# Four changes of queue, engine and order, and the per-head sums of squares of q and k in four column groups

## The chip, the cores and the metric

The kernel runs on one core of a Trainium2 chip. The metric is the device time of one execution in microseconds (us). A core has five engines that work side by side, each through its own instructions in order: TensorE (PE, matrix products; its weight loads are shown apart as PEld), VectorE (DVE), ScalarE (ACT), GpSimd (POOL) and SyncE (SP, which here only issues DMAs). They wait for each other by semaphores. DMAs are issued by SP and ACT (hardware queues) and by POOL (software queue).

## The reference

One decoder layer is computed in float32 for 1024 prompt tokens and 8 sample tokens (1032 columns), with model width 1024 and feed-forward width 2816. The outputs are the new activations and the new caches. Cut to what matters here:

```python
h = h + 0.5 * swiglu(rmsnorm(h, g_f1), w_f1_gu, w_f1_down)      # up 1, down 1
u = rmsnorm(h, g_mix) @ w_in                                     # the mixer's projections
q = rmsnorm(q.reshape(bsz, T, N_HEADS_A, HEAD_DIM), g_q) * (HEAD_DIM ** -0.5)   # per head of 64
k = rmsnorm(k.reshape(bsz, T, N_HEADS_A, HEAD_DIM), g_k)
mix = concat(attention(q, k, v), conv_module(glu), pool_mixer(c)) @ w_out
h = h + mix
h = h + 0.5 * swiglu(rmsnorm(h, g_f2), w_f2_gu, w_f2_down)      # up 2, down 2
```

The rmsnorm of q and k per head needs, for each of the 8 + 8 heads and each of the 1032 tokens, the sum of 64 squares.

## The kernel before

Activations lie transposed: a tile has 128 features on the partitions and tokens along the columns, either a half of 516 columns (`HF`), or a third of 344 (`CH`, `CW` = 344). A float32 product is made of three matmuls on high and low parts (`hi` on ACT by a copy that rounds, `lo` on DVE by a subtraction), and each stage streams its weights: a 256 KB load, a high part and a low part ("wop") for each 128x512 block.

The stages follow each other on PE: **up 1** (L512 to L514), **down 1** (L773 to L775), the **mixer** (projections L283 to L285, then the V blocks L1158 to L1160, with the convolution, the norms of q and k and the attention mixed in), **out-proj** (L283 to L285 again) and **up 2**, **down 2** (the same lines as up 1 and down 1). A scheduler that plans ahead of time turns the program into one fixed instruction order per engine; what is written later in the program with less to wait for can be placed earlier. Hardware DMAs rotate over eight completion slots, so a DMA waits until the one eight before it has landed; those of POOL have eight slots of their own.

*Up.* `up` works with seven products per feed-forward tile f (a Strassen-like scheme on two halves of the features and two halves of the tokens). Products 1 and 2 of the first f's ("early": 14 in up 1, 12 in up 2) need only the raw first half of the tokens, so they run first and their results are copied out of PSUM (`v`, ACT, L521) and kept in DRAM (L522). Product 2 of an f accumulates on product 1 in the same PSUM tile, and stands `lag` f's behind it; there are four such tiles of two banks. Meanwhile `norms()` squares the tokens (ACT, L405), sums the squares over the eight feature tiles on DVE (L407), and `total` sums over the partitions on PE (L388), then a root on ACT (L390) and a reciprocal on DVE (L391). The first halves of x are loaded by SP (L368); `fetch_x` (L380 to L382) loads the second halves, through POOL's queue, into buffers of 13 that rotate; the eighth waits until one comes free. In up 2 the lag is 3 (L888), and its early products are interleaved with the last of out-proj.

*Mixer.* For q and k, eight 128-row tiles are projected. `total` (L1116 to L1119) sums the squares of q tile p and k tile p with a 0/1 matrix `sel`: two matmuls of 344 columns, one into partitions 0 to 31 of `acc[c]`, one into 32 to 63; they accumulate over p = 0 to 3 in three banks (c = 0 to 2), so there are 12 such pairs. `side_v` (L1186 ff.) is a generator that advances one step per V block (16 blocks of 128 tokens by 256 columns). It scales the sums by r, takes root and reciprocal (`stat`, L1198 to L1202), splits the result into `rr` (high part on 64 partitions by ACT, low part on the other 64 by DVE), and `norm(t)` (L1217) spreads it with one product `bcx` x `rr` for each tile and third, and multiplies q or k by that on DVE. Between its steps `conv_tail` is advanced: the layer norm of the convolution, whose sums are matmuls against `ones` (L277) of the split `sh`, `sl` of the two convolution tiles `cy`. `xs` (L1064 to L1068), high plus low part of the eight sample columns, is added up by eight small POOL instructions.

*Out-proj.* Each of 16 steps adds the product to h (L933), stores the sum to `hd2` in DRAM through POOL's queue (L934) and squares it (L935). Up 2 reads `hd2` back.

Of the kernel before, what the change touches and what calls it, by code (L numbers as in the profile page):

```python
# [11 lines left out]
F32 = mybir.dt.float32  # L12
# [8 lines left out]
KT = D // P  # L21
SEQ = 1024
NS = 8
T = SEQ + NS
CW = T // 3
CH = [slice(i * CW, (i + 1) * CW) for i in range(3)]
HT = T // 2
# [159 lines left out]
class Trunk:  # L187
# [151 lines left out]
    def up(self, src, n, g, norm, lag, extra=iter(())):  # L339
# [39 lines left out]

        def fetch_x(k, hf):  # L380
            x = tmp(f"x{hf}")
            nc.gpsimd.dma_start(x, src(k, hf))  # L382
            return x
# [9 lines left out]
        def norms():  # L393
            if not norm:
                for _ in range(2):
                    yield
                total(1, self.tail)
                return
            accs = []
            xs = [fetch_x(k, 1) for k in range(HK)]  # L400
            for hf in range(2):
                acc = None
                for k in range(KT):
                    sq = xs[k] if hf else tmp("sq")
                    nc.scalar.activation(sq, sq if hf else first_x[k], AF.Square)  # L405
                    if k:
                        nc.vector.tensor_tensor(sq, sq, acc, op=ALU.add)  # L407
                    acc = sq
                    if k == HK - 1:
                        yield  # L410
                        if hf == 0:
                            xs += [fetch_x(i, 1) for i in range(HK, KT)]
                accs.append(acc)
                yield
            yield
            for hf in range(2):
                total(hf, accs[hf])
                yield
# [431 lines left out]
    def body(self):  # L850
# [32 lines left out]
        with contextlib.ExitStack() as right:  # L883
            with self.page_pools():
                with self.side_pools():
                    mh, ml = self.mixer(hd)
                self.x1p = right.enter_context(self.first_pool())
                gen = self.up(lambda k, hf: hd2[k][:, HF[hf]], 2, "g2", False, 3)  # L888
                self.out_proj(mh, ml, hd, hd2, gen)
# [7 lines left out]
    def out_proj(self, mh, ml, hd, hd2, ahead):  # L897
# [24 lines left out]
        for at, (hf, d) in enumerate(steps):  # L922
# [4 lines left out]
            for j in range(2):  # L927
# [5 lines left out]
                nc.vector.tensor_tensor(out, ps, out, op=ALU.add)  # L933
            nc.gpsimd.dma_start(hd2[d][:, HF[hf]], x)  # L934
            nc.scalar.activation(sq, x, AF.Square)  # L935
# [15 lines left out]
    def mixer(self, hd):  # L951
# [114 lines left out]
        for k in range(KT):  # L1066
            nc.gpsimd.tensor_tensor(xs[:, k], self.xh[k][:, SEQ:T].bitcast(F32), self.xl[k][:, SEQ:T].bitcast(F32),
                                    op=ALU.add)  # L1068
# [17 lines left out]

        acc = [self.ps()[:, :CW] for _ in range(3)]
        qk = [None] * 8
        wv = None
        pool = self.pool_tail(pooled)  # L1090
        for p in range(4):
# [7 lines left out]
            for c in range(3):  # L1099
# [16 lines left out]
                def total(c=c, p=p, parts=parts):  # L1116
                    for e in range(2):
                        nc.tensor.matmul(acc[c][32 * e:32 * e + 32], sel[:, 32 * p:32 * p + 32], parts[e],
                                         start=p == 0, stop=p == 3)  # L1119

# [63 lines left out]
    def side_v(self, conv, qk, acc, gq, smq):  # L1184
# [9 lines left out]
        yield  # L1194
        sc = [self.t("stat")[0:64] for _ in range(3)]
        for c in range(3):
            r = self.r[0:64, CH[c]]
            nc.vector.tensor_tensor(sc[c], acc[c][0:64], r, op=ALU.mult)  # L1198
            nc.vector.tensor_tensor(sc[c], sc[c], r, op=ALU.mult)
            nc.scalar.activation(sc[c], sc[c], AF.Sqrt, bias=self.eps[0:64])  # L1200
            nc.vector.reciprocal(sc[c], sc[c])
            nc.vector.tensor_tensor(sc[c], sc[c], r, op=ALU.mult)  # L1202
        tail = self.conv_tail()
        next(tail, None)
        yield
        for c in range(3):
            self.hi(rr[0:64, CH[c]], sc[c])
            self.lo(rr[64:128, CH[c]], sc[c], rr[0:64, CH[c]])
        next(tail, None)
        yield  # L1210
        next(tail, None)
        yield

# [486 lines left out]
```

## Time and profile before

| | |
|---|---|
| three timed runs | 1853.35, 1855.25, 1856.14 us, median 1855.25 |
| the profiled execution | 1856.26 us, of which the profile's span is 1854.5 us |
| mean granted PE clock | 0.996 of 2.4 GHz |
| busy: PE, DVE, ACT, POOL | 98%, 72%, 39%, 12% of the span |
| the chain that ended last | PE 90%, DVE 4%, DMA 3%, ACT 2%, issue 1% |

The page says how busy each engine is. With PE busy for 98% of the span, what can be won is in the few gaps where PE waits, in the stretches that run at half clock, and in the work that PE does. The view of the waits lists the gaps by the engine and line waited for; the timeline of an engine shows each instruction with its start, its duration and in brackets the idle time before it.

### The profile page before, as it was taken

To read this page: it belongs to the slowest core of one execution; us is meant where nothing else is said; L and a number is where in the kernel's file an instruction comes from. 1 tells how busy PE (TensorE), PEld (TensorE's weight loads), DVE (VectorE), ACT (ScalarE), POOL (GpSimd) and SP (SyncE) were. 2 spreads that over 40 slices of the span, in tenths; PEclk is the share of its full clock that TensorE was granted. 3 is DMA by queue.
4 is the path that set the end of the run, shared out by engine and by line. 5 is a ranking of instruction groups with operands and counts; after the bars stand their busy time and mean duration, and the time that the engine had idled before them with its cause. 6 is when DMAs were issued, how large, how long until landed. Compare 5 with 4: busy or idle time off the path is not lost.

```text
span 1854.5 us, 35895 instructions
## 1 busy us (share of the span) xinstructions
PE 1822.7 (98%) x14436; PEld 1750.0 (94%) x14436; DVE 1343.4 (72%) x2140; ACT 724.7 (39%) x1307; POOL 213.4 (12%) x205
## 2 busy tenths in 40 slices
PE   7999999999999999999899999999999999999999
PEld 7999999999999999998865689989999999999999
DVE  6877787778686566997666755577777877868654
ACT  6532222322333455235655653443222222243342
POOL 2100000000000004732532423200000000000000
PEclk9999999999999999999999999999999999999999
DMA  9544365454964243212353256654433435596421
GB/s 330 195 139 149 115 182 191 144 183 161 327 244 118 84 158 94 53 38 75 121 159 115 93 170 207 216 169 158 131 127 111 142 120 181 168 325 245 117 81 46
DMA packets 155578, 286.72 MB, mean 155 GB/s; under 512 B 25992, under 2 KB 32732, under 8 KB 155412
## 3 DMA queue, kind: packets, MB, share of 16 engines
q1 hardware_dynamic: 116276, 206.21, 35.7%
q10 hardware_dynamic: 34560, 63.20, 9.1%
q0 software_dynamic: 4576, 15.01, 2.4%
q8 instruction: 113, 1.85, 0.4%
q14 instruction: 53, 0.43, 0.1%
HBM read 208.29 MB, written 78.61 MB: 155 GB/s over the span
## 4 chain that ended last, share of the span: by engine, by line
PE 90%; DVE 4%; DMA 3%; ACT 2%; issue 1%; SPq 0%; ACTq 0%; DVEq 0%
PE ps L512 15%; PE ps L513 15%; PE ps L514 15%; PE ps L773 8%; PE ps L774 8%; PE ps L775 8%; PE ps L283 5%; PE ps L284 5%; PE ps L285 5%; PE ps L1599 2%; PE ps L1580 1%; DMA wr<-wgu 1%; PE ps L1527 1%; DVE pt L1530 1%; PE ps L1528 1%; PE ps L1159 1%
## 5 line engine op out<-in xcount | busy, mean ns | idle before, releaser
L512 PE MATMUL ps<-xot,wop 128*128 128x258 f32 x1408 | 396.3, 283 | 1.8 <-DVE v L565 1.8
L513 PE MATMUL ps<-xot,wop 128*128 128x258 f32 x1408 | 397.9, 283 | 0.0
L514 PE MATMUL ps<-xot,wop 128*128 128x258 f32 x1408 | 397.0, 282 | 0.0
L773 PE MATMUL ps<-mop,wop 128*128 128x258 f32 x1232 | 348.1, 283 | 0.9 <-DVE v L578 0.9
L774 PE MATMUL ps<-mop,wop 128*128 128x258 f32 x1232 | 347.4, 282 | 0.0
L775 PE MATMUL ps<-mop,wop 128*128 128x258 f32 x1232 | 346.6, 282 | 0.0
L512 PE MATMUL ps<-xo,wop 128*128 128x258 f32 x1056 | 301.3, 286 | 6.1 <-ACT v L521 3.9
L513 PE MATMUL ps<-xo,wop 128*128 128x258 f32 x1056 | 300.0, 284 | 0.0
L514 PE MATMUL ps<-xo,wop 128*128 128x258 f32 x1056 | 299.6, 284 | 0.4 <-DVE wop L244 0.4
L512 PEld LDWEIGHTS ps<-xot,wop 128*128 128x128 f32 x1408 | 265.1, 189 | 2.9 <-issue 2.6
L513 PEld LDWEIGHTS ps<-xot,wop 128*128 128x128 f32 x1408 | 265.8, 189 | 1.5 <-issue 1.5
L514 PEld LDWEIGHTS ps<-xot,wop 128*128 128x128 f32 x1408 | 265.9, 189 | 0.0
L774 PEld LDWEIGHTS ps<-mop,wop 128*128 128x128 f32 x1232 | 233.5, 190 | 0.0
L773 PEld LDWEIGHTS ps<-mop,wop 128*128 128x128 f32 x1232 | 232.2, 189 | 1.1 <-issue 1.1
L775 PEld LDWEIGHTS ps<-mop,wop 128*128 128x128 f32 x1232 | 232.7, 189 | 0.0
L241 ACT ACTIVATE wop<-s 128x512 fp32r<-128x512 f32 x176 | 105.8, 628 | 292.6 <-DVE s L478 227.9
L512 PEld LDWEIGHTS ps<-xo,wop 128*128 128x128 f32 x1056 | 201.1, 191 | 9.0 <-ACT v L521 5.5
L514 PEld LDWEIGHTS ps<-xo,wop 128*128 128x128 f32 x1056 | 201.2, 191 | 0.9 <-DVE wop L244 0.8
L513 PEld LDWEIGHTS ps<-xo,wop 128*128 128x128 f32 x1056 | 201.4, 191 | 0.3 <-DVE xo L374 0.2
L244 DVE TENSOR_TENSOR wop<-wr,wop 128x512 fp32r<-128x512 f32 x180 | 121.7, 696 | 55.1 <-ACT wop L241 54.9
L244 DVE TENSOR_TENSOR wop<-s,wop 128x512 fp32r<-128x512 f32 x176 | 117.7, 688 | 36.1 <-ACT wop L241 35.6
L241 ACT ACTIVATE wop<-wr 128x512 fp32r<-128x512 f32 x180 | 107.2, 622 | 89.1 <-PE ps L775 76.7
(263 smaller groups left out, 3404.8 us busy)
## 6 DMA issues: line engine op xcount, KB each, us to landing
wr<-wgu SPq DMA_DIRECT2D x227, 256.0 KB
mt<-v ACTq DMA_DIRECT2D x88, 258.0 KB
mr<-mt SPq DMA_DIRECT2D x88, 258.0 KB
m<-v ACTq DMA_DIRECT2D x66, 258.0 KB
mr<-m SPq DMA_DIRECT2D x66, 258.0 KB
kept<-v ACTq DMA_DIRECT2D x52, 258.0 KB
v<-kept SPq DMA_DIRECT2D x52, 258.0 KB
h<-hd SPq DMA_DIRECT2D x48, 258.0 KB
```

The source lines that it names most:

```text
L241: self.nc.scalar.activation(out, src, AF.Copy)
L244: (eng or self.nc.vector).tensor_tensor(out, src, hi.bitcast(F32), op=ALU.subtract)
L283: mm(out, wh, xh, start=i == 0, stop=False)
L284: mm(out, wh, xl, start=False, stop=False)
L285: mm(out, wl, xh, start=False, stop=i == n - 1)
L512: mm(out, wh, xh, start=start and k == 0, stop=False)
L513: mm(out, wh, xl, start=False, stop=False)
L514: mm(out, wl, xh, start=False, stop=stop and k == HK - 1)
L773: mm(out, wh, mh, start=opens, stop=False)
L774: mm(out, wh, ml, start=False, stop=False)
L775: mm(out, wl, mh, start=False, stop=closes)
L1599: mm(O[half[e], q1 - w:q1], vt[j // 2][:, j % 2, hc:hc + 64], pT[:, e, :], start=j == 0, stop=j == 2 * b + 1)
```

## The change

1. In up 1, `norms()` loads the second half of x (eight loads) through SP's queue; every other user of `fetch_x` stays on POOL's.
2. In up 2 the lag is 2, not 3.
3. The 16 stores of out-proj into `hd2` are issued by ACT.
4. The eight additions of `xs` are done by DVE.
5. `total` for q and k makes four matmuls of 172 columns, into the four groups of 32 partitions of `acc[c]`: q and k, first half of the third and second half. The statistics then stand on 128 partitions by 172 columns: root and reciprocal are one instruction each per third as before, with half the columns; the multiplications with r are made by 64 partitions; the high part goes into a tile `stath` first and from there by two copies on ACT to `rr`; the low part is two subtractions. `conv_tail` is still advanced once with the statistics, and then four times before the first norm where it was twice; `rr` is written just ahead of the first of these four, so each norm stands two V blocks later.

```diff
-        def fetch_x(k, hf):
+        def fetch_x(k, hf, queue=nc.gpsimd):
             x = tmp(f"x{hf}")
-            nc.gpsimd.dma_start(x, src(k, hf))
+            queue.dma_start(x, src(k, hf))
...
-            xs = [fetch_x(k, 1) for k in range(HK)]
+            xs = [fetch_x(k, 1, nc.sync) for k in range(HK)]
...
-                            xs += [fetch_x(i, 1) for i in range(HK, KT)]
+                            xs += [fetch_x(i, 1, nc.sync) for i in range(HK, KT)]
...
-                gen = self.up(lambda k, hf: hd2[k][:, HF[hf]], 2, "g2", False, 3)
+                gen = self.up(lambda k, hf: hd2[k][:, HF[hf]], 2, "g2", False, 2)
...
-            nc.gpsimd.dma_start(hd2[d][:, HF[hf]], x)
+            nc.scalar.dma_start(hd2[d][:, HF[hf]], x)
...
-            nc.gpsimd.tensor_tensor(xs[:, k], self.xh[k][:, SEQ:T].bitcast(F32), self.xl[k][:, SEQ:T].bitcast(F32),
+            nc.vector.tensor_tensor(xs[:, k], self.xh[k][:, SEQ:T].bitcast(F32), self.xl[k][:, SEQ:T].bitcast(F32),
...
-        acc = [self.ps()[:, :CW] for _ in range(3)]
+        acc = [self.ps()[:, :CH2] for _ in range(3)]
...
-                    for e in range(2):
-                        nc.tensor.matmul(acc[c][32 * e:32 * e + 32], sel[:, 32 * p:32 * p + 32], parts[e],
-                                         start=p == 0, stop=p == 3)
+                    for g in range(4):
+                        nc.tensor.matmul(acc[c][32 * g:32 * g + 32], sel[:, 32 * p:32 * p + 32],
+                                         parts[g % 2][:, g // 2 * CH2:(g // 2 + 1) * CH2],
+                                         start=p == 0, stop=p == 3, skip_group_check=True)
...
-        sc = [self.t("stat")[0:64] for _ in range(3)]
+        sc = [self.t("stat") for _ in range(3)]
+        half = [slice(0, 64), slice(64, 128)]
...
         for c in range(3):
-            r = self.r[0:64, CH[c]]
-            nc.vector.tensor_tensor(sc[c], acc[c][0:64], r, op=ALU.mult)
-            nc.vector.tensor_tensor(sc[c], sc[c], r, op=ALU.mult)
-            nc.scalar.activation(sc[c], sc[c], AF.Sqrt, bias=self.eps[0:64])
-            nc.vector.reciprocal(sc[c], sc[c])
-            nc.vector.tensor_tensor(sc[c], sc[c], r, op=ALU.mult)
+            x = sc[c][:, 0:CH2]
+            for h in range(2):
+                nc.vector.tensor_tensor(x[half[h]], acc[c][half[h]], self.r[half[h], cols(c, h)], op=ALU.mult)
+                nc.vector.tensor_tensor(x[half[h]], x[half[h]], self.r[half[h], cols(c, h)], op=ALU.mult)
+            nc.scalar.activation(x, x, AF.Sqrt, bias=self.eps)
+            nc.vector.reciprocal(x, x)
+            for h in range(2):
+                nc.vector.tensor_tensor(x[half[h]], x[half[h]], self.r[half[h], cols(c, h)], op=ALU.mult)
...
         for c in range(3):
-            self.hi(rr[0:64, CH[c]], sc[c])
-            self.lo(rr[64:128, CH[c]], sc[c], rr[0:64, CH[c]])
-        next(tail, None)
-        yield
-        next(tail, None)
-        yield
+            x, xh = sc[c][:, 0:CH2], self.t("stath", dt=F32R)[:, 0:CH2]
+            self.hi(xh, x)
+            for h in range(2):
+                nc.scalar.activation(rr[0:64, cols(c, h)], xh[half[h]].bitcast(F32), AF.Copy)
+                self.lo(rr[64:128, cols(c, h)], x[half[h]], xh[half[h]])
+        for _ in range(4):
+            next(tail, None)
+            yield
```

Lines of the changed kernel stand 1 lower than before from the top, 2 lower at the statistics' first lines and 11 lower from `norm` on (L407 is L408, L1217 is L1228).

Three places in the order move. The first is DVE in up 1, around the sums of squares of the second half of x (`x_289` to `x_345`, each x its own buffer; `sq` are the sums of the first half; `wop` the low parts of weights). Before:

```order
L407 TENSOR_TENSOR x_339<-x_339,x_293 128x516
L244 TENSOR_TENSOR wop<-wr,wop 128x512 x2
L407 TENSOR_TENSOR x_341<-x_341,x_339 128x516
L391 RECIPROCAL r<-sd 128x516
L244 TENSOR_TENSOR wop<-wr,wop 128x512 x2
L407 TENSOR_TENSOR x_343<-x_343,x_341 128x516
L244 TENSOR_TENSOR wop<-wr,wop 128x512 x2
L407 TENSOR_TENSOR x_345<-x_345,x_343 128x516
L391 RECIPROCAL r<-sd 128x516
```

After, at the same place:

```order
L408 TENSOR_TENSOR x_339<-x_339,x_293 128x516
L408 TENSOR_TENSOR x_341<-x_341,x_339 128x516
L245 TENSOR_TENSOR wop<-wr,wop 128x512
L408 TENSOR_TENSOR x_343<-x_343,x_341 128x516
L245 TENSOR_TENSOR wop<-wr,wop 128x512
L408 TENSOR_TENSOR x_345<-x_345,x_343 128x516
L245 TENSOR_TENSOR wop<-wr,wop 128x512
L392 RECIPROCAL r<-sd 128x516
L245 TENSOR_TENSOR wop<-wr,wop 128x512 x4
L392 RECIPROCAL r<-sd 128x516
```

The last sum now stands ahead of the first reciprocal, and two low parts, not six, stand between `x_339` and it.

The second is SP's queue at the start (`x_174` to `x_186` are the first halves of x, `v` the kept products read back). Before:

```order
L368 DMA x_183<-x 128x516 x2
L368 DMA x_186<-x 128x516 x2
L465 DMA wr<-wgu 128x512 x38
L532 DMA v_1357<-kept_0_158 128x516
L532 DMA v_1359<-kept_0_158 128x516
```

After, from the last of the seven loads of x that follow the first nine weight loads:

```order
L383 DMA x_343<-x 128x516
L466 DMA wr<-wgu 128x512 x2
L383 DMA x_345<-x 128x516
L466 DMA wr<-wgu 128x512 x27
L533 DMA v_1357<-kept_0_158 128x516
```

The eight loads of x stand among the weights, and 27 weight loads stand behind the eighth.

The third is ACT in `side_v`, from the load of the root's table on (`stat` the root, `misc` and `v` belong to the V blocks, `sh` the convolution's high parts, `rr` the statistics' high parts). Before:

```order
L241 ACTIVATE sh<-cy_8947 128x344
L1165 ACTIVATE misc<-ps 128x1
L1200 ACT_TABLE_LOAD
L1200 ACTIVATE stat<-stat,eps 64x344
L241 ACTIVATE sh<-cy_9462 128x344
L1166 ACTIVATE v_10030<-ps,misc 128x256
L241 ACTIVATE wboth<-wr 128x512
L1200 ACTIVATE stat<-stat,eps 64x344
L241 ACTIVATE sh<-cy_8947 128x344
```

After:

```order
L1208 ACT_TABLE_LOAD
L1208 ACTIVATE stat<-stat,eps 128x172 x3
L1167 ACTIVATE misc<-ps 128x1
L1168 ACTIVATE v_10048<-ps,misc 128x256
L1167 ACTIVATE misc<-ps 128x1
L1168 ACTIVATE v_10049<-ps,misc 128x256
L242 ACTIVATE stath<-stat 128x172
L1219 ACTIVATE rr<-stath 64x172 x2
L242 ACTIVATE stath<-stat 128x172 x2
L242 ACTIVATE sh<-cy_8947 128x344
```

The first `sh` stood ahead of the table load; it now stands behind the three `stath`, which need the statistics' last multiplications. On PE the matmul that reads this `sh` still stands right behind the third V block; the first norm (L1217, now L1228) moved from behind the fourth V block to behind the sixth.

## Rows read from the trace of the kernel before

**Rows 1.** Engines' busy time, from the page: us, share of the span, instructions.

```profile
PE 1822.7 (98%) x14436; PEld 1750.0 (94%) x14436; DVE 1343.4 (72%) x2140; ACT 724.7 (39%) x1307; POOL 213.4 (12%) x205
```

**Rows 2.** Waits of PE: line, waited-for engine and line, us, times, longest.

```profile
PE ps L388 <- DVE x L407: 5.7, 1, 5.7
PE ps L1217 <- DVE rr L244: 5.5, 3, 4.0
PE ps L512 <- ACT v L521: 3.9, 8, 0.7
```

**Rows 3.** Timeline of PE in up 1: start, duration, instruction, idle before.

```profile
35.56 0.28 PE L514 MATMUL ps<-xo,wop 128*128 128x258 f32 x1
41.58 2.06 PE L388 MATMUL ps<-x,mat 128*128 128x258 f32 x4 [5.74 <-DVE x L407]
```

**Rows 4.** Windows: stretch, busy time and count by engine, granted PE clock, DMA share, GB/s.

```profile
core 0: us, PE busy (x) PEld busy (x) DVE busy (x) ACT busy (x) POOL busy (x), PEclk, DMA share, GB/s
10.00:20.00 10.00, 9.84 (x71) 9.61 (x70) 5.93 (x9) 6.39 (x12) 0.81 (x2) 1.00 1.04 390
40.00:50.00 10.00, 8.42 (x46) 8.08 (x47) 5.59 (x6) 1.81 (x3) 1.07 (x2) 0.66 0.53 177
886.60:893.60 7.00, 5.44 (x20) 4.71 (x21) 4.80 (x8) 3.67 (x7) 3.86 (x4) 0.51 0.26 91
```

**Rows 5.** Timeline of DVE in up 1, around the sums of x.

```profile
32.58 0.69 DVE L407 TENSOR_TENSOR x<-x,x 128x516 f32<-128x516 f32 x1
...
34.50 3.38 DVE L391 RECIPROCAL r<-sd 128x516 f32<-128x516 f32 x1 [1.23 <-ACT sd L390]
...
40.75 0.69 DVE L407 TENSOR_TENSOR x<-x,x 128x516 f32<-128x516 f32 x1
```

**Rows 6.** Timelines of ACT and POOL in up 1: a copy out, the eighth load.

```profile
30.82 0.60 ACT L521 ACTIVATE v<-ps 128x516 f32<-128x516 f32 x1
...
19.57 0.54 POOL L382 DMA_DIRECT2D x<-x  x1 [9.20 <-DVE sq L407]
```

**Rows 7.** DMA issues on POOL's queue: count, KB each, median us to landing.

```profile
x<-x POOLq DMA_DIRECT2D x24, 258.0 KB, 5.3
hd<-h POOLq DMA_DIRECT2D x16, 258.0 KB, 3.6
```

**Rows 8.** Timeline of PE: a pair of sums of squares, and four column groups.

```profile
850.74 0.77 PE L1118 MATMUL ps<-sq,sel 128*32 128x344 f32 x4
851.44 0.42 PE L283 MATMUL ps<-dh,wboth 128*128 128x344 f32 x1
...
957.38 0.59 PE L1400 MATMUL ps<-kt,qs 128*32 128x225 f32 x8
957.90 0.44 PE L1527 MATMUL ps<-k,qs 128*128 128x384 f32 x1
```

**Rows 9.** Groups by line: weight loads of L1400, count, busy us, mean ns, idle.

```profile
L1400 PEld LDWEIGHTS ps<-kt,qs 128*32 128x32 f32 x64 | 1.4, 108 | 2.4 <-issue 1.0 <-DVE kt L1387 0.8 <-DVE mt L244 0.4
```

**Rows 10.** Timeline of PE in the V blocks.

```profile
878.59 0.42 PE L277 MATMUL ps<-sh,ones 128*128 128x344 f32 x1
...
886.62 0.66 PE L1217 MATMUL ps<-rr,bcx 128*128 128x344 f32 x1 [3.98 <-DVE rr L244]
```

**Rows 11.** Timelines of ACT and DVE in the V blocks.

```profile
874.38 0.47 ACT L241 ACTIVATE sh<-cy 128x344 fp32r<-128x344 f32 x1
...
875.07 1.28 ACT L1200 ACT_TABLE_LOAD   x1
...
876.98 2.29 DVE L1201 RECIPROCAL stat<-stat 64x344 f32<-64x344 f32 x1 [3.71 <-ACT stat L1200]
...
882.17 0.44 DVE L1202 TENSOR_TENSOR stat<-stat,r 64x344 f32<-64x344 f32 x1
```

**Rows 12.** The chain that ended last, at the end of out-proj; PE behind it.

```profile
1176.37 5.96 DMA hd<-h
1182.44 2.58 ACT xo L373 x4
...
1186.07 0.39 PE L512 MATMUL ps<-xo,wop 128*128 128x258 f32 x1 [0.94 <-ACT wop L241]
```

**Rows 13.** Timeline of POOL: the eight additions of xs.

```profile
700.62 8.69 POOL L1067 TENSOR_TENSOR xs<-xh,xl 128x8 f32<-128x8 f32 x8 [20.74 <-DVE xl L296]
```

More of the change, by code (lines that the diff above doesn't have):

```diff
@@ L25 @@
 CW = T // 3
+CH2 = CW // 2
 CH = [slice(i * CW, (i + 1) * CW) for i in range(3)]
@@ L1194, in side_v, with cols @@
         yield
-        sc = [self.t("stat")[0:64] for _ in range(3)]
+        sc = [self.t("stat") for _ in range(3)]
+        half = [slice(0, 64), slice(64, 128)]
+        def cols(c, h):
+            return slice(c * CW + h * CH2, c * CW + (h + 1) * CH2)
         for c in range(3):
-            r = self.r[0:64, CH[c]]
-            nc.vector.tensor_tensor(sc[c], acc[c][0:64], r, op=ALU.mult)
-            nc.vector.tensor_tensor(sc[c], sc[c], r, op=ALU.mult)
-            nc.scalar.activation(sc[c], sc[c], AF.Sqrt, bias=self.eps[0:64])
-            nc.vector.reciprocal(sc[c], sc[c])
-            nc.vector.tensor_tensor(sc[c], sc[c], r, op=ALU.mult)
+            x = sc[c][:, 0:CH2]
[6 more added lines that the diff above has]
+                nc.vector.tensor_tensor(x[half[h]], x[half[h]], self.r[half[h], cols(c, h)], op=ALU.mult)
         tail = self.conv_tail()
```

## The prediction, made before the changed kernel ran

> **What bounds the kernel now.** I read the engines' busy times first: PE is busy for 1822.7 of 1854.5 us [rows 1], so a change can win only where PE waits, where it runs at half clock, or in PE's own work. The waits of PE come next. Three of the first four lines are at places that this change touches: 5.7 us in up 1 for the last sum of squares of x, 5.5 us in the V blocks for `rr`, and 3.9 us in eight pieces in up 2 for PSUM tiles to be copied out [rows 2]. The windows then show what a long wait costs beyond itself: the granted clock is 0.66 of 2.4 GHz from 40 to 50 us, and 0.51 from 886.6 to 893.6 us, so after each of the two long waits PE goes on at 1.2 GHz for some microseconds [rows 4]. From 40 to 50 the missing clock is 0.34 x 10 = 3.4 us, of which 0.8 falls on the wait itself; so about 2.4 to 2.6 us are lost by slow matmuls behind the first wait. In the V blocks it is 0.49 x 7 = 3.4 us, less 0.8 for two short waits in it: 2.6 us.
>
> **Up 1: the loads of x and the order on DVE.** PE arrives at the second L388 at 35.84 and waits until 41.58 [rows 3]. The sum it needs ends at 41.4 on DVE, and the 3.38 us of the first reciprocal, which that sum does not need, stand in front of it, between 32.58 and 40.75, with four low parts of weights [rows 5]. In the new order all eight sums stand before the first reciprocal, with two low parts after the fifth sum. What then holds the last sum is ACT: its square of the eighth tile stands just behind a copy out that ended at 31.4 before [rows 6]. Square 0.6, sum 0.7 and a low part that may lie ahead 0.6: about 33.7 us, 2 us before PE arrives. So the wait of 5.74 goes, and with it the half clock behind it, 2.4: **-8.1 us**. What is late next is nothing that I find: PE then takes a weight tile of 24 matmuls each 2.8 us, and the order has 14 low parts ahead of the first reciprocal against 8 used by then, so the reciprocal of 3.38 hides.
>
> The loads must come in time. Ahead of the last of the x loads in SP's queue stand 8 first halves, 13 weight tiles and 7 second halves, about 7.6 MB with it; the stretch from 10 to 20 us moved 390 GB/s [rows 4], so they are in at about 21 us, or 25 to 27 for the eighth, which waits for a buffer that a sum of squares frees, at 19.57 before [rows 6], and took 5.3 us to land in the median [rows 7]. Its square comes at 31.4. The 27 weight loads wait behind it; the first was needed by ACT about 30. The margin is 4 us. The bounds: 0 if that margin is gone and PE waits as long as before, -9.6 if the short wait of 1.5 for the first half's squares goes too, which I don't expect, since its last sum now stands behind three of x.
>
> **Up 2: lag and store.** With lag 3, three PSUM tiles stay open between the two products of an f and the fourth must be copied out before PE goes on: eight waits, 3.9 us [rows 2]. With lag 2 there is one tile more in hand, and a copy of 0.6 us [rows 6] has a whole product of 24 matmuls to hide behind. They go: -3.9. The store of the last h into `hd2` takes 5.96 us to land and is on the chain; its buffer or its data release the next `xo`, and PE waits 0.94 behind it [rows 12]. The median of the same stores is 3.6 us [rows 7]; on ACT's queue it need only be 1 us faster than 5.96 for that 0.94 to go. Together **-4.8 us**; bounds -6, if PE's slow restarts after each wait go too, and -1, if the eight waits turn into waits for weights that are now needed earlier. The 16 issues on ACT cost about 0.35 us each on an engine that is busy for 39% [rows 1]; I take them at nothing. If ACT had no gap there, PE would pay some 0.3 us at two or three steps, 1 us in all.
>
> **xs on DVE.** POOL took 8.69 us for eight tiny additions, and nobody waited for them [rows 13]; on DVE they are some 0.13 us each by the smallest DVE operations near by, an estimate, 1 us in all. PE has whole projections to do meanwhile: 0. Were DVE the limit there, +1.
>
> **Column groups.** A pair of 344-column matmuls holds PE from 850.74 to 851.44, 0.70 us; a set of four in four groups, 225 columns each, 0.52 us [rows 8]. Both are float32 on 128 rows by 32 columns, and the second already is what the change makes of the first, only wider. The difference is 0.18 us for 119 columns, 1.5 ns per column; 172 columns are then 0.52 - 0.08 = 0.44, against 0.70. Twelve pairs, none hidden, since PE does not wait there: 12 x 0.26 = **-3.1 us**. In proportion to the columns a set would be 0.40 (-3.6); if four groups gained nothing over two, 0.
>
> **The wait in the V blocks is moved, not removed.** The norms stand two V blocks, some 7 us, later than the 886.62 at which the first one could begin [rows 10], and `rr` is ready before. But the matmul on `sh` is still behind the third V block, where it stood without a wait at 878.59 [rows 10], and its `sh`, which ACT had done at 874.85, ahead of the table load at 875.07 [rows 11], now stands behind the three `stath`. These wait for three reciprocals and six multiplications on DVE. The first reciprocal begins about 876.4: it was 876.98 [rows 11], the sums are in 0.7 earlier, `sh` is no longer in front, a copy of V and a high part of weights are instead. A reciprocal of 516 columns takes 3.38 [rows 5], of 344 columns 2.29 [rows 11], so 6.3 ns per column, and 1.2 us for 172; three end at 880.0. A multiplication of 64x344 is 0.44 [rows 11], so half as many columns between 0.22 and 0.44, I take 0.27; six end at 881.6. A `stath` 0.3 and `sh` 0.47: 882.4. PE arrives at 877.9. It waits 4.5 us where it waited 5.5, and goes on at half clock as before: **-1.0 us**. With the cheapest prices the wait is 4.0, with the dearest 5.8: -1.5 to +0.3.
>
> **Sum.** -8.1 - 4.8 - 3.1 - 1.0 = -17.0. The profiled execution took 1856.26, which gives 1839.3; the median of the three timed runs is 1.0 lower, so I forecast **1838.3 us**.
>
> **The rivals.** *The start gives back.* The x loads are now in one queue with the weights and share its eight slots; if one that is needed lands 4 us later than I think, PE waits 2 to 6 us as before. Against it: the margin above. For it: the DMA engines are full until 30 us, so that delays add up. Half the term gone gives 1842, all of it 1846.4. Chance 0.19.
>
> *Four groups bring nothing.* The 64 weight loads of L1400, 108 ns each, which would be 6.9 us in a row, took 1.4 us [rows 9]: loads into different column groups overlap in this trace. The Trainium skill, TensorE: Matmul & The Clock Gate, section "The mechanism" of Part 3, says that a weight load overlaps with running matmuls only if it goes to another row group; the four groups here share all rows. By that rule the eight loads of a set would stand in a row; these rows speak against it. As a mechanism of this kernel: eight loads of 0.108 are 0.86 us instead of 0.70, +1.9 over twelve sets instead of -3.1, which gives 1843.3. Chance 0.06.
>
> *The waits of up 2 stay.* Product 2 of an f comes one step earlier and its weights too; if each of the eight waits becomes one of the same size for a weight part, 1842.2. Chance 0.09.
>
> *The V wait shrinks below what halves the clock.* With the clock kept, 2.6 us more are won, and with `sh` in time all 7: 1831 to 1836. Against it: the order on ACT. Chance 0.12.
>
> *Slower.* With the software queue gone from the start, only eight transfers are in flight, some 2.1 MB. At 390 GB/s that needs each to land within 5.4 us, as it did. If the landing got longer and the rate fell, the 7.6 MB would hold the last sum: below 230 GB/s PE waits again, below 160 GB/s (landing after 13 us) the whole gain of 17 us is gone, and at 130 GB/s the last x is in at 59 us, PE waits 25, and the kernel takes 1866. Nothing in the trace shows transfers that slow, so the chance is 0.04.
>
> **Chances.** The forecast 0.47, the rivals as above 0.50, the rest 0.03 for something that I don't see. About 0.2%, 3.7 us, is what a measurement of this kernel can tell from no change. To end within that, two of the terms must fail together: 0.06; slower 0.05; faster 0.89. The range 1830.5 to 1846.5 reaches from a V wait that goes wholly to a start that brings nothing.
>
> **What would show it.** Step by step in the profile of the changed kernel: no wait of L388 for x of over 1 us and a clock of 1.00 from 36 to 50 us; no L512 that waits for `v` in up 2, and none of over 0.5 for `wop` near 1170; 0.40 to 0.45 from a set of sums of squares to the next matmul; one wait of 4 to 6 us of L278 for `sh` on ACT about 870, a clock near 0.5 behind it, and none of L1228 for `rr`. It is wrong if L388 still waits for x or if new waits for weights stand in the first 60 us, and most wrong if the V blocks show no wait at all or one of over 8 us.

## The result, and the profile after

The changed kernel takes 1834.46 us in the median of four runs (1833.09 to 1836.73), beside 1855.70 for the kernel before in the same comparison. The ratio is 0.9889, with a 95% interval of 0.9871 to 0.9906: by it 20.6 us less, between 17.4 and 23.9. The forecast was 17.0 less, to 1838.3, in a range of 1830.5 to 1846.5. The time lies in the range and the direction is right; some 4 us more were won than the sum said, and the places show where. One execution of a kernel below (1914.74 us, at a granted clock of 0.878) and one of the kernel before (4502.28 us) lie far above the others of their kernels and are left out of every median and ratio.

The page of the changed kernel has PE busy in 1811.9 of 1833.1 us, 10.8 us less than in [rows 1], and about 21 us of idle time where it was 32:

```profile
span 1833.1 us, 35972 instructions
...
PE 1811.9 (99%) x14484; PEld 1745.9 (95%) x14484; DVE 1341.7 (73%) x2160; ACT 726.1 (40%) x1313; POOL 191.0 (10%) x173
```

The waits of PE answer to [rows 2]. Of the three lines there none is left; a wait for `sh` has come in, the longest that there is now:

```profile
PE ps L278 <- ACT sh L242: 6.8, 1, 6.8
PE ps L513 <- DVE v L566: 2.2, 3, 0.9
PE ps L1610 <- DVE pT L1598: 1.6, 4, 0.6
PE ps L513 <- ACT wop L242: 1.6, 1, 1.6
...
PE ps L513 <- DVE h L934: 0.5, 1, 0.5
```

*Up 1.* The first view is PE's timeline, the second DVE's. Both L389 now run without a wait, the one for x at 32.86, where before it started at 41.58 [rows 3]; the last sum of x ends at 30.1, and the first reciprocal comes behind it (before, it stood in front of it, [rows 5]):

```profile
26.49 1.03 PE L389 MATMUL ps<-sq,mat 128*128 128x258 f32 x4
32.86 1.03 PE L389 MATMUL ps<-x,mat 128*128 128x258 f32 x4
```

```profile
25.36 0.69 DVE L408 TENSOR_TENSOR sq<-sq 128x516 f32<-128x516 f32 x1
...
29.39 0.70 DVE L408 TENSOR_TENSOR x<-x,x 128x516 f32<-128x516 f32 x1
...
31.91 3.38 DVE L392 RECIPROCAL r<-sd 128x516 f32<-128x516 f32 x1 [1.22 <-ACT sd L391]
```

The windows (stretch, busy time and count of PE, PEld, DVE, ACT and POOL, granted clock, DMA share, GB/s) have no half clock left at 36 to 50 us, where the row of before, for 40 to 50, has 0.66 [rows 4]; the second stretch is the one behind the wait in the V blocks, at 1.2 GHz:

```profile
36.00:50.00 14.00, 14.00 (x119) 14.00 (x118) 13.97 (x19) 7.69 (x14) 2.13 (x5) 1.00 0.98 342
871.00:875.00 4.00, 3.80 (x17) 3.80 (x18) 2.08 (x5) 3.44 (x10) 2.96 (x4) 0.50 0.00 0
```

*Column groups.* On PE's timeline a set of four takes 0.43 us to the next matmul, where a pair took 0.70 [rows 8]:

```profile
847.03 0.50 PE L1119 MATMUL ps<-sq,sel 128*32 128x172 f32 x8
847.46 0.43 PE L284 MATMUL ps<-xh,whi 128*128 128x344 f32 x1
```

*V blocks.* PE's timeline, then ACT's, then DVE's. The matmul on `sh` waits 6.76 us behind the third V block, in place of the 3.98 and two shorter ones for `rr` [rows 10]; the chain to it is the table load, the root, three reciprocals, six products, `stath`, `sh`:

```profile
864.06 0.38 PE L1166 MATMUL ps<-mat,r 1*128 1x1 f32 x2
871.20 0.66 PE L278 MATMUL ps<-sh,ones 128*128 128x344 f32 x1 [6.76 <-ACT sh L242]
```

```profile
861.62 0.42 ACT L1194 ACTIVATE bcx<-bcr 128x256 fp32r<-128x256 f32 x1 [1.72 <-DMA bcr<-c_bc]
...
863.28 1.28 ACT L1208 ACT_TABLE_LOAD   x1
...
869.01 0.35 ACT L242 ACTIVATE stath<-stat 128x172 fp32r<-128x172 f32 x1 [2.21 <-DVE stat L1211]
...
870.68 0.47 ACT L242 ACTIVATE sh<-cy 128x344 fp32r<-128x344 f32 x1
```

```profile
865.04 3.40 DVE L1209 RECIPROCAL stat<-stat 128x172 f32<-128x172 f32 x3 [2.20 <-ACT stat L1208]
868.36 2.03 DVE L1211 TENSOR_TENSOR stat<-stat,r 64x172 f32<-64x172 f32 x6
```

*Where the time went.* The same instructions can be found in both traces by the view of one line's instructions (first and last start). Their distance tells how much is won up to there:

| up to | before | after | won so far |
|---|---|---|---|
| second L388 (L389), up 1 | 41.6 | 32.9 | 8.7 |
| first L832 (L833), up 1 | 157.6 | 146.4 | 11.2 |
| first L283 (L284), mixer | 692.5 | 682.1 | 10.4 |
| first L1118 (L1119) | 789.5 | 778.5 | 11.0 |
| first V block, L1158 (L1160) | 866.7 | 853.3 | 13.4 |
| first L1400 (L1411), behind the V blocks | 947.1 | 933.2 | 13.9 |
| last product of out-proj, L283 (L284) | 1175.1 | 1160.6 | 14.5 |
| last `xo` product, end of up 2 (L512, L513) | 1628.0 | 1606.7 | 21.3 |
| span | 1854.5 | 1833.1 | 21.4 |

So the start gave 11.2 (8.1 forecast), nine of the twelve sets 2.4 and, with the last three, 3.2 (3.1), and out-proj with up 2 6.8 (4.8). From the first norm of a V block (871.61 before, 857.38 after) to the first L1400 both kernels take 75.5 to 75.8 us: the V blocks lost 0.3 (a gain of 1.0 was forecast). What is left, between these places, comes to some 0.5 and is not followed up here.

### The profile page after: what moved, and what is told of

Same layout as the page of the kernel before. It is cut to its first block, busy times and chain, and to the rows that moved or that the text cites. A ratio compares the mean times of both kernels' runs of the same rounds, so it can differ in the third digit from the quotient of the medians.

```text
span 1833.1 us, 35972 instructions
## 1 busy us (share of the span) xinstructions
PE 1811.9 (99%) x14484; PEld 1745.9 (95%) x14484; DVE 1341.7 (73%) x2160; ACT 726.1 (40%) x1313; POOL 191.0 (10%) x173
## 3 DMA queue, kind: packets, MB, share of 16 engines
q8 instruction: 114, 1.87, 0.4%
## 4 chain that ended last, share of the span: by engine, by line
PE 94%; DVE 3%; DMA 1%; issue 1%; ACT 1%; SPq 0%; DVEq 0%; ACTq 0%
PE ps L513 16%; PE ps L514 16%; PE ps L515 16%; PE ps L774 8%; PE ps L776 8%; PE ps L775 8%; PE ps L284 5%; PE ps L285 5%; PE ps L286 5%; PE ps L1610 2%; PE ps L1591 1%; PE ps L1538 1%; DVE pt L1541 1%; PE ps L1539 1%; PE ps L1161 1%; PE ps L1160 1%
## 5 line engine op out<-in xcount | busy, mean ns | idle before, releaser
L513 PE MATMUL ps<-xot,wop 128*128 128x258 f32 x1408 | 395.9, 283 | 2.2 <-DVE v L566 2.2
L513 PE MATMUL ps<-xo,wop 128*128 128x258 f32 x1056 | 299.8, 284 | 2.1 <-ACT wop L242 1.6
L513 PEld LDWEIGHTS ps<-xot,wop 128*128 128x128 f32 x1408 | 264.9, 189 | 3.3 <-issue 2.6
L513 PEld LDWEIGHTS ps<-xo,wop 128*128 128x128 f32 x1056 | 200.0, 189 | 3.1 <-ACT wop L242 2.3
```

What stands on the lines that cost most here:

```text
L513: mm(out, wh, xh, start=start and k == 0, stop=False)
```

## The experiments

Ten kernels ran. All are the changed kernel with one thing different, but for three that start from the kernel before, and each was timed in five rounds beside the kernel before on the same chip. The ratios are to that. The last column is the difference of two medians that were not taken side by side.

| kernel | median us | ratio to before, 95% | against the changed kernel, us |
|---|---|---|---|
| changed kernel | 1834.46 | 0.9889 (0.9871 to 0.9906) | |
| x through POOL's queue again | 1847.33 | 0.9957 (0.9944 to 0.9971) | +12.9 |
| last four loads of x on POOL's queue | 1839.43 | 0.9922 (0.9909 to 0.9936) | +5.0 |
| lag 3 again | 1840.80 | 0.9922 (0.9908 to 0.9935) | +6.3 |
| stores on POOL's queue again | 1835.37 | 0.9895 (0.9880 to 0.9911) | +0.9 |
| xs on POOL again | 1834.04 | 0.9888 (0.9875 to 0.9902) | -0.4 |
| the four repairs without the column groups | 1836.67 | 0.9900 (0.9884 to 0.9916) | +2.2 |
| the column groups without the repairs | 1851.98 | 0.9986 (0.9977 to 0.9994) | +17.5 |
| repairs, old groups, norms two V blocks later | 1829.48 | 0.9864 (0.9850 to 0.9877) | -5.0 |
| bcr through POOL's queue | 1833.53 | 0.9886 (0.9872 to 0.9900) | -0.9 |
| rr written three steps later | 1827.10 | 0.9845 (0.9832 to 0.9857) | -7.4 |

The ratios' intervals are 1.6 to 3.3 us wide to either side, and the runs of one kernel lie 2 to 6 us apart. A difference of about 1 us can't be told from none by these times, and one of 2 us only together with the trace.

**The first repair, undone.**

```diff
-            xs = [fetch_x(k, 1, nc.sync) for k in range(HK)]
+            xs = [fetch_x(k, 1) for k in range(HK)]
...
-                            xs += [fetch_x(i, 1, nc.sync) for i in range(HK, KT)]
+                            xs += [fetch_x(i, 1) for i in range(HK, KT)]
```

> The changed kernel with only the first repair undone: the second half of x comes through POOL's queue again. Theory A (the order on DVE and the short wait for the first half's squares are both due to this repair): about 11 us slower than the changed kernel, near 1845.5, with a wait of L389 for x of 5 to 6 us, one of about 1.5 for the first half's squares, and half clock after the long one. Theory B (the prediction's term: the long wait and its half clock alone): 8 us slower, near 1842.5, and the short wait stays away. Rival C (the gain at the start comes from something else, such as the moment at which the clock first rises): under 3 us slower.

It is 12.9 us slower, and 11.4 to 14.2 by its single runs, nearer to theory A than to B. The trace is of one of the two longer runs (1848.14 us). The long wait is back with its old length and its place behind the reciprocal. The short wait is not back under its own name; in its stead PE waits for weights at 16.7 us. First the waits, then PE's timeline:

```profile
PE ps L389 <- DVE x L408: 5.7, 1, 5.7
PE ps L513 <- ACT wop L242: 3.9, 2, 2.0
```

```profile
16.73 0.39 PE L513 MATMUL ps<-xo,wop 128*128 128x258 f32 x1 [1.87 <-ACT wop L242]
17.45 0.57 PE L515 MATMUL ps<-xo,wop 128*128 128x258 f32 x1 [0.22 <-DVE wop L245]
...
43.07 2.06 PE L389 MATMUL ps<-x,mat 128*128 128x258 f32 x4 [5.74 <-DVE x L408]
```

ACT waits three times there for weight loads (13.97, 16.04 and 17.87, 1.1 to 1.4 us each); in the changed kernel it doesn't. From 10 to 20 us the DMA engines move 390 GB/s here and 383 in the changed kernel, which points to whose bytes go first: with x in a queue of its own, its seven loads, issued at 6.5 to 10.2 us, travel beside the weights; in SP's queue they come behind nine weight loads, at 13.8 to 17.6. The Trainium skill, DMA: Bandwidth & Descriptors, section "Queues, rings and completion order", says that a DMA engine takes turns between the queues that have work for it and takes one queue's descriptors in order; the traces agree, since ACT has three such waits, of 1.1 to 1.4 us, in each of the three kernels that load all of x through POOL's queue, this one, the kernel before and the one with the column groups alone.

How much of that reaches PE differs between executions of the same order. Here PE waits 2.1 us for weights, with the column groups alone 1.0, and in the kernel before 0.2 (at 15.93). The second L389 starts at 43.07 here, at 41.84 with the column groups alone, and at 41.58 in the kernel before [rows 3]:

```profile
41.84 2.06 PE L389 MATMUL ps<-x,mat 128*128 128x258 f32 x4 [5.75 <-DVE x L408]
```

So theory A is right on what returns, but for the short wait, and some 1.3 us of this trace are spread between executions and not the price of the queue.

**Half of the first repair.** The first four loads stay in SP's queue, the last four go to POOL's. In DVE's order one sum then stands behind the first reciprocal, not two or none.

```diff
-                            xs += [fetch_x(i, 1, nc.sync) for i in range(HK, KT)]
+                            xs += [fetch_x(i, 1) for i in range(HK, KT)]
```

> The changed kernel with the last four of the eight loads of x on POOL's queue; the first four stay on SP's, behind nine weight loads. In DVE's order one sum, the last, now stands behind the first reciprocal (3.38 us), where in the changed kernel none does and with all eight on POOL's queue two do. Theory A (what the wait of L389 costs is set by what stands ahead of the last sum on DVE): the last sum ends some 3 to 4 us later, PE waits 2.5 to 4 us for x, and runs at half clock behind it if the wait is long enough: 3 to 6 us slower than the changed kernel, 1837.5 to 1840.5. Rival B (the queue sets it, the loads on POOL's queue take the engines from the weights): waits for weights of 1 us or more at 10 to 18 us as with all eight on POOL's, and the same long wait, 9 us slower or more. Rival C (PE has slack there): within 1.5 us.

Theory A. It is 5.0 us slower. On DVE the last sum is behind the reciprocal, and PE waits until it ends; the short wait for the first half's squares is back too, at 1.03. ACT waits twice for weight loads (0.80 and 1.43 us), but PE waits for none. PE's timeline, then DVE's:

```profile
28.57 1.11 PE L389 MATMUL ps<-sq,mat 128*128 128x258 f32 x4 [1.03 <-DVE sq L408]
38.45 1.11 PE L389 MATMUL ps<-x,mat 128*128 128x258 f32 x4 [3.03 <-DVE x L408]
```

```profile
34.38 3.38 DVE L392 RECIPROCAL r<-sd 128x516 f32<-128x516 f32 x1 [1.15 <-ACT sd L391]
37.67 0.63 DVE L408 TENSOR_TENSOR x<-x,x 128x516 f32<-128x516 f32 x1
```

So the place of the reciprocal in DVE's order makes the long wait, and the queue matters by what it does to that order, and by the weights' share. Behind this wait of 3.03 the granted clock stayed at 1.00 (38 to 50 us), where behind the 5.74 of before it was 0.66 from 40 to 50 [rows 4]: no half clock came on top.

**The lag, undone.**

```diff
-                gen = self.up(lambda k, hf: hd2[k][:, HF[hf]], 2, "g2", False, 2)
+                gen = self.up(lambda k, hf: hd2[k][:, HF[hf]], 2, "g2", False, 3)
```

> The changed kernel with lag 3 in up 2 again. Theory A (a wait of PE costs its idle time and about 0.27 us more, because the running matmul drains and the next one starts without one in front of it): eight waits of 0.45 to 0.7 cost 5.8 us, near 1840.3. Theory B (a wait costs the idle time that the view of the waits shows): 3.9 us, near 1838.4. Rival C (the store's queue, not the lag, ended the eight waits): no eight waits, within 1 us of the changed kernel.

Theory A: 6.3 us slower, with the eight waits of 3.9 us in all. What a wait costs beyond that stands in PE's timeline:

```profile
1195.59 0.28 PE L515 MATMUL ps<-xo,wop 128*128 128x258 f32 x1
1196.47 0.39 PE L513 MATMUL ps<-xo,wop 128*128 128x258 f32 x1 [0.60 <-ACT v L522]
```

Matmuls of this shape follow each other every 0.12 us. The one at 1196.47 would have come at 1195.71 and is 0.76 late, of which the view calls 0.60 idle, because the matmul before it is counted as busy for its whole 0.28; and the restarted one takes 0.1 longer to the next. So a wait costs some 0.26 us more than its bracket, and eight of them 3.9 + 2.1 = 6.0. The other waits of the eight show the same surplus.

**The stores, undone.**

```diff
-            nc.scalar.dma_start(hd2[d][:, HF[hf]], x)
+            nc.gpsimd.dma_start(hd2[d][:, HF[hf]], x)
```

> The changed kernel with out-proj's stores on POOL's queue again. Theory: the last store lands about 6 us after its issue, PE waits 0.9 for the high part of weights where it waited 0.5 for the last h, with the drain 0.5 to 1 us slower, 1835 to 1835.5, and no wait for copies out in up 2. Rival (the store's queue is what brought more than the term in up 2): 2 us slower or more.

As the theory said, 0.9 us slower, at the edge of what can be told. The trace has the wait for weights, which the changed kernel doesn't have, on PE; a wait of 0.5 for the last h is in both:

```profile
1171.21 0.39 PE L513 MATMUL ps<-xo,wop 128*128 128x258 f32 x1 [0.63 <-ACT wop L242]
1171.94 0.39 PE L515 MATMUL ps<-xo,wop 128*128 128x258 f32 x1 [0.23 <-DVE wop L245]
```

**xs, undone.**

```diff
-            nc.vector.tensor_tensor(xs[:, k], self.xh[k][:, SEQ:T].bitcast(F32), self.xl[k][:, SEQ:T].bitcast(F32),
+            nc.gpsimd.tensor_tensor(xs[:, k], self.xh[k][:, SEQ:T].bitcast(F32), self.xl[k][:, SEQ:T].bitcast(F32),
```

> The changed kernel with the eight additions of xs on POOL again. Theory: nobody waits for them, within 1 us of the changed kernel; a wait for the low part of x in the projections is 0.6 to 1.3 us either way. Rival: the POOL instructions of some 9 us hold up the work of DVE and the first projections, 2 us slower.

No difference: -0.4 us, and the wait for the low part of x is 0.7 us with either. It is 0.7 too in the kernel with lag 3 and 1.3 where x comes through POOL's queue, so its change from 1.3 is not due to `xs`.

**The four repairs alone, and the column groups alone.** The first is the kernel before with changes 1 to 4, the second the kernel before with change 5.

> The kernel before with the first four repairs and the old sums of squares (two groups of 344 columns, statistics on 64 partitions, norms where they were). Theory A (the four column groups save 0.27 us in each of twelve sets, and the wait in the V blocks only changed its place): 2 to 3.5 us slower than the changed kernel, near 1837.3, with 0.70 us from a pair of sums to the next matmul, and waits of L1217 for rr of some 5.5 us. Rival (the new statistics and the later norms are worth more than the matmuls): 6 us slower or more.

> The kernel before with the fifth change alone: four column groups, the statistics on 128 partitions, the norms two V blocks later. Theory A (twelve sets, each 0.27 us shorter, and a wait for sh in place of one for rr, of 5 to 7 us by where the loads of bcr land): 1.5 to 3.5 us faster than the kernel before, 1852 to 1854, all four waits that the repairs are for as long as before. Rival (the five changes help each other, so that the fifth alone gives nothing or its whole gain depends on the others): within 0.5 us of the kernel before, or over 5 us faster.

Both as theory A has it. Without the column groups it is 2.2 us slower than the changed kernel; a pair takes 0.71 us, and the old waits for `rr` are there. The column groups alone win 0.14% (0.06 to 0.23), 2.6 us, with the old waits of up 1 and up 2 at their old length beside the new one for `sh`. The four repairs together are worth 17.5 us with the column groups and 18.5 without; undone one at a time they add up to 19.7, so no large part of the gain comes from two of them together. PE's timeline and its waits in the kernel with the repairs alone:

```profile
803.22 0.77 PE L1118 MATMUL ps<-sq,sel 128*32 128x344 f32 x4
803.93 0.43 PE L283 MATMUL ps<-xh,whi 128*128 128x344 f32 x1
```

```profile
PE ps L1217 <- DVE rr L244: 5.6, 3, 3.8
```

and the waits in the one with the column groups alone:

```profile
PE ps L278 <- ACT sh L242: 6.0, 1, 6.0
PE ps L389 <- DVE x L408: 5.7, 1, 5.7
PE ps L513 <- ACT v L522: 3.9, 8, 0.7
```

**The wait in the V blocks.** Three kernels ask what sets it. In the first, the new position of the norms is given to the old statistics:

```diff
-        next(tail, None)
-        yield
-        next(tail, None)
-        yield
+        for _ in range(4):
+            next(tail, None)
+            yield
```

> As the kernel before with the first four repairs and the old sums of squares, but with four steps of the convolution's tail ahead of the first norm where there were two: the norms stand two V blocks later, and the sh stay ahead of the statistics on ACT. Theory A (the wait in the V blocks is a matter of what stands where, not of the column groups): no wait of L277 for sh and at most 1 us for rr, no half clock in the V blocks, 1828 to 1830, that is faster than the changed kernel although each pair of sums still takes 0.70. Rival (DVE is the limit in this stretch, so that the wait comes up at the next product instead): within 2 us of the kernel with the four repairs alone, 1835 to 1839.

Theory A: 1829.48 us, 7.2 less than with the repairs alone and 5.0 less than the changed kernel, with the old pairs of 0.70. PE waits in the V blocks neither for `sh`, which stays ahead of the statistics on ACT, nor for `rr`:

```profile
867.82 0.38 PE L1164 MATMUL ps<-mat,r 1*128 1x1 f32 x2
868.13 0.42 PE L277 MATMUL ps<-sh,ones 128*128 128x344 f32 x1
...
880.04 0.73 PE L1216 MATMUL ps<-rr,bcx 128*128 128x344 f32 x3
```

In the second, the changed kernel's `stath` and `rr` are written ahead of the last of the four steps of the tail, not the first (three steps later; the expectation says two), so that no `sh` of these steps is left behind them:

```diff
-        for c in range(3):
-            x, xh = sc[c][:, 0:CH2], self.t("stath", dt=F32R)[:, 0:CH2]
...
-        for _ in range(4):
+        def spread():
+            for c in range(3):
+                x, xh = sc[c][:, 0:CH2], self.t("stath", dt=F32R)[:, 0:CH2]
...
+        for step in range(4):
+            if step == 3:
+                spread()
             next(tail, None)
             yield
```

> The changed kernel with one block of code moved: the high and low parts of the statistics (stath, rr) are written two steps of the convolution's tail later, so that no sh stands behind a stath on ACT. Theory A: the wait of 5 to 7 us for sh goes with the half clock behind it, no wait of the norms for rr, 8 to 9 us faster than the changed kernel, near 1826. Rival 1: rr is now late for the first norm, a wait of some 4 us takes its place, 1830 to 1832. Rival 2 (something else of that stretch is late behind it): within 2 us.

Theory A again, with a little less: 1827.10 us, 7.4 under the changed kernel and 28 under the kernel before. Beside the kernel with four steps and the old groups it is 2.4 faster, so with no such wait on either side the column groups bring about what they bring in the two pairs above (2.2 and 2.6). The matmul on `sh` follows the third V block at once, the first norm has its `rr`, and PE is busy throughout. Its timeline and a window:

```profile
863.25 0.38 PE L1166 MATMUL ps<-mat,r 1*128 1x1 f32 x2
863.56 0.42 PE L278 MATMUL ps<-sh,ones 128*128 128x344 f32 x1
...
875.45 0.73 PE L1232 MATMUL ps<-rr,bcx 128*128 128x344 f32 x3
```

```profile
860.00:880.00 20.00, 20.00 (x152) 19.23 (x153) 16.93 (x32) 15.07 (x41) 13.33 (x15) 1.00 0.20 76
```

The third asks why the wait was 6.76 and not the forecast 4.5. The copies `bcx` stand ahead of the table load on ACT and wait for their loads `bcr`; here these go through POOL's queue.

```diff
-            nc.sync.dma_start(bcr[:, 0:256], io["c_bc"][:, 2 * i:2 * i + 2].rearrange("p a b -> p (a b)"))
+            nc.gpsimd.dma_start(bcr[:, 0:256], io["c_bc"][:, 2 * i:2 * i + 2].rearrange("p a b -> p (a b)"))
```

> The changed kernel with the four loads of bcr, whose copies stand on ACT ahead of the root of the statistics, on POOL's queue and not on SP's. Theory A (the wait for sh came out longer than forecast because these loads land late, so ACT reaches the table load late): the table load starts 1.5 to 3 us earlier as seen from the third V block, the wait for sh falls to 3 to 5 us, 1 to 3 us faster, near 1832.5. Rival (the reciprocals and the products behind them alone set the wait): the wait stays at 5 to 7 us, within 1 us.

Between the two: the table load comes 2.0 us ahead of the third V block's norm where it was 0.8 ahead, and the wait falls by 0.83 to 5.93, and not by 1.2, since one `bcx` (0.4) now stands between the first two roots. The time, 0.9 us less, can't be told from none. ACT and PE:

```profile
861.08 1.28 ACT L1208 ACT_TABLE_LOAD   x1
```

```profile
863.07 0.38 PE L1166 MATMUL ps<-mat,r 1*128 1x1 f32 x2
869.37 0.65 PE L278 MATMUL ps<-sh,ones 128*128 128x344 f32 x1 [5.93 <-ACT sh L242]
```

The other kernels tell more, since those with the new statistics in their place all have this wait, and their loads land at other times. Start of the table load less start of the third V block's norm (ACT's and PE's timeline), and the wait:

| kernel | table load | norm | difference | wait | wait less difference |
|---|---|---|---|---|---|
| changed kernel | 863.28 | 864.06 | -0.78 | 6.76 | 7.54 |
| x on POOL's queue | 875.28 | 876.07 | -0.79 | 6.76 | 7.55 |
| column groups alone | 872.72 | 874.24 | -1.52 | 6.03 | 7.55 |
| lag 3 | 863.25 | 865.12 | -1.87 | 5.69 | 7.56 |
| xs on POOL | 861.75 | 863.73 | -1.98 | 5.57 | 7.55 |
| last four of x on POOL's queue | 866.99 | 867.93 | -0.94 | 6.62 | 7.56 |
| stores on POOL's queue | 861.60 | 863.95 | -2.35 | 5.21 | 7.56 |

The last column is the same each time: with the 0.38 that the norm itself takes, 7.9 us lie between the start of the table load and the matmul on `sh`. What differs is when ACT reaches the table load. It starts 1.66 or 1.67 us behind the start of the last copy `bcx` in all seven, and where the view shows that copy by itself, in six, it has waited for its load, 0.7 to 1.9 us.

## Why the prediction was right, and where its numbers were off

- **What bounds the kernel**: right. What was won lies on PE: its waits, the half clock behind them, the twelve sets and some 0.5 us of an earlier full clock at the start.
- **Up 1, the long wait**: right in mechanism and size. The wait of 5.74 and the half clock went; the last sum came at 30.1, earlier than the 33.7 worked out, since the copy out that I set ahead of the last square was earlier too. The run with half of the loads moved ties the wait to the reciprocal's place.
- **Up 1, the rest**: the step that failed is "-9.6 if the short wait of 1.5 for the first half's squares goes too, which I don't expect". It went: their last sum ended at 26.05 on DVE, PE came to it at 26.49. I had looked at what is new ahead of that sum, not at how much earlier ACT begins the squares (15.67, against 17.39 in the trace of before). Counted from when PE was due, the short wait had cost 1.6 us, and the long one 6.2, half a us more than its bracket: the two L388 lie 12.6 us apart before and 6.4 now. The half clock behind it was worth 2.5 in place of 2.4. The last 0.9 lies ahead of the first L388, due at 27.34 before and reached at 26.49 now. Of that, some 0.4 is the wait for weights at 15.93 in the trace of before; the other 0.5 is that matmuls come every 0.12 us from 12.8 on before and from 11.8 on now, and every 0.22 just ahead of that. The working had neither, and whether the change moves the clock's rise is not shown (last section). Together these are the 3 us between 8.1 and 11.2.
- **The loads' margin**: right. SP issued the eighth at 19.70, and PE waited for none of them. The rival in which the start gives back did not come about, nor the slow one: the queues moved 383 GB/s from 10 to 20 us.
- **Up 2**: right in mechanism, the term mis-sized. I took the eight waits at the 3.9 us of their brackets; they cost 6.0, since each is some 0.26 longer on PE than its bracket; the bound of -6 allowed for that, the term did not. Of the lag and the store, the first is worth 6.3 and the second about 0.9.
- **xs**: nothing, as said; on DVE an addition takes 0.16 us, where 0.13 was estimated.
- **Column groups**: 0.43 against the 0.44 worked out, 3.2 us against 3.1. The last three sets stand in a row and take 1.01 us, where three pairs took 1.86. The rival by which weight loads into the same rows don't overlap is wrong here: by the groups by line the set's eight weight loads, 108 ns each, took 2.1 us for all 96, not 10.4:

```profile
L1119 PEld LDWEIGHTS ps<-sq,sel 128*32 128x32 f32 x96 | 2.1, 108 | 2.1 <-issue 1.9
```

- **V blocks**: right that the wait is moved and not removed, and that it waits for `sh`. Off by 2.3 us: the step "The first reciprocal begins about 876.4" put it 1.5 us ahead of PE's arrival, and it began 0.6 behind it. From there to the end of `sh` I had 6.0 us, and it took 6.1. What was missing is that the copies of `bcx` ahead of it wait for loads, and that these need not move with the sums: the last began 2.4 us behind the first V block's norm before, and 2.7 to 4.2 behind it in the kernels above. The wait also went past the dearest price, 5.8, and yet the V blocks lost only 0.3: from 871 to 878 us the clock is 0.69, so the half clock cost 2.2 us where it was 2.6. The rest of that is not taken apart here.
- **The sum**: the terms were 3.1 and 2.0 too little and 1.3 too much, so that part of the errors cancelled by luck. The range is 16 us wide, and the time would have lain in it without that.

## What to carry to other kernels

A wait that is moved is not won: ask of each instruction that the new order puts ahead of another what it waits for, and who waits behind it; here one block of code written three steps later was worth 7.4 us, more than twice the column groups that brought it. Price a wait of PE by the start of the next matmul against when it was due, not by the idle time in brackets, and add the half clock behind a long one. When a load moves to another queue, look at two things: whose bytes it now travels ahead of, and what the scheduler does with the work behind it.

## What the runs showed of the hardware that I had not expected

A wait of PE costs about 0.26 us beyond its bracket, in these shapes: 0.16 by the matmul that drains, 0.1 by the one that restarts.

The moment at which PE's clock first rises is not the same in two runs of the same instructions. From 10 to 12 us PE did 17 matmuls in the kernel with `xs` on POOL and 11 in the one with lag 3, whose orders of PE, ACT and DVE are the same there; matmuls come every 0.12 us from 10.2 on in the first and from 13.2 in the second, and every 0.22 just ahead of that. The first L389 then stands at 25.8 and at 27.1 us. In the eight kernels that load all of x through SP's queue the second stands at 32.3 to 33.5. So about 1 us of the start, and of any difference between two runs, can be chance. Where weights are late, an earlier rise need not help: with the column groups alone it came at 10.7, 2.1 us earlier than in the kernel before, and PE then waited 1.0 us for weights and reached its first L389 0.25 us later than that kernel its first L388. The windows of the kernel with `xs` on POOL and of the one with lag 3, in this order:

```profile
10.00:12.00 2.00, 2.00 (x17) 2.00 (x17) 2.00 (x5) 1.96 (x4) 0.00 (x0) 1.00 1.05 389
```

```profile
10.00:12.00 2.00, 2.00 (x11) 2.00 (x11) 2.00 (x5) 1.99 (x4) 0.00 (x0) 1.00 1.05 386
```

The granted clock is given as 1.00 for both, so in these first microseconds the spacing of the matmuls tells the two apart, and the row's clock does not.
